# A hybrid gMLP and Mamba-2 layer on one core: low parts of the first operands on other engines, z tiles fetched one segment earlier, one norm three steps later

## Chip, core and metric

The kernel runs on one core of a Trainium2 chip. The metric is the device time of one execution in microseconds (us), taken on the core. Five engines work side by side, each with its own queue of instructions in a fixed order: TensorE (PE in the profile, its weight loads PEld), VectorE (DVE), ScalarE (ACT), GpSimd (POOL) and SyncE (SP), which here issues most of the DMAs.

## What is computed

One layer of a diffusion backbone on 2048 tokens of width 1024 with 256 context tokens, all in fp32:

```python
def _rms(x):
    x32 = x.astype(jnp.float32)
    y = x32 * lax.rsqrt(jnp.mean(x32 * x32, axis=-1, keepdims=True) + EPS)
    return y.astype(x.dtype)
...
    proj = h @ (w_in if with_output else w_in[:, 2 * GM_WIDTH:])
    ssd_in = proj[..., proj.shape[-1] - SSD_IN_WIDTH:]
    z, xbc, dt_raw = jnp.split(ssd_in, [SSD_WIDTH, SSD_WIDTH + CONV_CH], axis=-1)
    xbc = jax.nn.silu(_conv_centred(xbc, conv_w, conv_b))
```

A root-mean-square norm with a scale and a shift from the conditioning vector (adaLN) gives the operand h. One projection of h feeds a gated MLP and a bidirectional Mamba-2 scan over chunks of 128 tokens; the output of the scan is multiplied by the gate silu(z) and normed. A second projection, a gated residual, another adaLN norm, a SwiGLU feed-forward part with a hidden width of 2816, a second gated residual and a last norm with its own weight follow. The context tokens give only the states from which the scans start.

## The kernel before

Activations lie with the channels on the partitions, in tiles of 128 channels by 512 tokens. The 2048 tokens are two blocks of two such columns of tiles, so a block has two halves of 512 tokens. A product in fp32 is made of three matmuls on parts: each operand is split into a high part (rounded to the format that TensorE takes at full rate, fp32r) and a low part (the rest), and high by high, high by low and low by high are added in a PSUM bank (`mm3`, L228 to L231 where the low parts come late, L234 to L236 otherwise). Three PSUM banks (`mmp`) take the products of a unit of weights, five (`smp`) take the rest.

**Start (to about 100 us).** The block worked on first has halves x2 (tiles `x2s`) and x3 (`x3s`), and the context comes beside it (`hc`). For each of the eight tiles of a half, `put` (L985 to L988) makes the operand pair `actt`: ScalarE writes the high part, scale times x plus shift (L986); GpSimd writes the same in full fp32 over x (L987); VectorE subtracts the high part and writes the low part (L988). The norm of x3 needs the sum of eight squares: ScalarE squares (L316), GpSimd adds seven times (L318), TensorE sums over partitions with a matrix of ones (L322), ScalarE takes Ln and Exp (L252, L253), VectorE refines (L254 to L256), and x3 is multiplied by the result (L1009) ahead of its own `put`. Then TensorE works through units of weights with the two halves and the context: a unit's bank for one half takes 16 matmuls of high parts and 8 with the low part of the activation (L231).

**Scan stage (about 800 to 1530 us).** `y_out` is a generator in segments, run for 32 pairs of chunk and head group, with other generators between the segments: matmuls and first sums, then the adds, then the gate: a DMA brings the z tile (L822), VectorE multiplies (L823), ScalarE squares and sums along the row (L824). TensorE transposes the result (L831). Products of the output projection run in between; VectorE takes their banks (L932).

**Second feed-forward product and last norm.** `ffn2` goes through seven phases of 11 steps (12 matmuls in a step), phase 3 last but one and phase 4 last. Half 1 is complete after phase 3, half 0 after phase 4. VectorE adds the banks to the residual tile (L1289), which SP has loaded (L1287); squares are summed (L261, L264), and `final` (L1329 on) does the norm: ones matmul (L1332), Ln and Exp, eight products (L1336) and eight stores (L1337). `final` of half 1 is called a number of steps after phase 3 has ended, `due`, in the middle of phase 4.

A tile framework gives each engine its queue: what the program writes is taken through a scheduler that fixes the order of instructions on every engine before the run, and places the waits on semaphores. The order on the chip is then that of the queues.

Of the kernel before, what the change touches and what calls it, by code (L numbers as in the profile page):

```python
# [7 lines left out]
F32 = mybir.dt.float32  # L8
F32R = mybir.dt.float32r
I32 = mybir.dt.int32  # L10
AF = mybir.ActivationFunctionType
ALU = mybir.AluOpType
# [9 lines left out]
TB = 512  # L22
# [61 lines left out]
def kernel(ctx: ExitStack, tc: tile.TileContext, xT, ctxp, cc, crow, wad1, wad2, vecs, rows,  # L84
                             gmb, wall, wdt, gmw, csts, outT, dbg=None):
    nc = tc.nc
    V, S, G, PE, DMA = nc.vector, nc.scalar, nc.gpsimd, nc.tensor, nc.sync
# [16 lines left out]
    def tma():  # L104
        return tpa.tile([P, 520], F32, name="tma", tag="tma")
# [9 lines left out]
    def mmp():  # L115
        return psm.tile([P, TB], F32, name="mmp", tag="mmp")

    def smp():
        return pss.tile([P, TB], F32, name="smp", tag="smp")

    def actt():
        return ap_.tile([P, 2, TB], F32R, name="actt", tag="actt")

    def bc(ap, n):
        return ap.broadcast_to(list(ap.shape[:-1]) + [n])
# [4 lines left out]
    zscr = [tc.dram_tile([P, D], F32, name=f"zscr{i}") for i in range(NCH)]  # L130
# [179 lines left out]
        return hs  # L310

    def sum_sq(xs, n, eng=V):
        acc = None
        for x in xs:
            sq = tma()
            S.activation(sq[:, :n], x, AF.Square)  # L316
            if acc is not None:
                eng.tensor_tensor(out=acc[:, :n], in0=acc[:, :n], in1=sq[:, :n], op=ALU.add)  # L318
            else:
                acc = sq  # L320
        ps = smp()
        PE.matmul(ps[:, :n], lhsT=ones, rhs=acc[:, :n], start=True, stop=True)  # L322
        return rstd_of(ps, n, tma)
# [18 lines left out]
    x3s = [x3t[k // 2][:, (k % 2) * TB:(k % 2 + 1) * TB] for k in range(KT)]  # L342
# [9 lines left out]
    def scale(xs, rb, n, eng):  # L352
        for x in xs:
# [14 lines left out]
        out=a1, in0=m_sb[:, 8:16, :], scalar=1.0,  # L368
        in1=bc(vec[:, V_N1:V_N1 + 8].rearrange("p (a o) -> p a o", o=1), 2), op0=ALU.add, op1=ALU.mult)
# [3 lines left out]
                    scalar1=0.5, scalar2=None, op0=ALU.mult)  # L373
# [312 lines left out]
    zdone = [0]  # L686
# [110 lines left out]
    def y_out(st, c, g, ms):  # L797
        rc, Gt, hb = st["rc"], st["G"], st["hb"]
        h = hst[(0, g)]
        py, pf, pb = smp(), smp(), smp()  # L800
        PE.matmul(pf, lhsT=rc[:, R_C:R_C + P], rhs=h, start=True, stop=True)
        PE.matmul(pb, lhsT=rc[:, R_C:R_C + P], rhs=hb, start=True, stop=True)
        for e in range(8):
            PE.matmul(py[:, e * HD:(e + 1) * HD], lhsT=Gt[e // 4][:, (e % 4) * P:(e % 4 + 1) * P],
                      rhs=rc[:, R_X + e * HD:R_X + (e + 1) * HD], start=True, stop=True)
        ya, yb = tma()[:, :TB], hb
        V.tensor_tensor(out=h3(ya), in0=h3(pf), in1=hv(eac[:, c, g * 8:g * 8 + 8]), op=ALU.mult)
        V.tensor_tensor(out=h3(yb), in0=h3(pb), in1=hv(eac[:, c, 16 + g * 8:16 + g * 8 + 8]), op=ALU.mult)
        yield
        if c < NCH - 1:  # L810
            pS = smp()
            PE.matmul(pS, lhsT=rc[:, R_B:R_B + P], rhs=st["xd"], start=True, stop=True)
            G.tensor_tensor(out=h3(h), in0=h3(h), in1=hv(tot[:, c, g * 8:g * 8 + 8]), op=ALU.mult)
            V.tensor_tensor(out=h, in0=h, in1=pS, op=ALU.add)
        V.tensor_tensor(out=ya, in0=ya, in1=yb, op=ALU.add)
        V.tensor_tensor(out=ya, in0=ya, in1=py, op=ALU.add)
        G.tensor_tensor(out=h3(yb), in0=h3(rc[:, R_X:R_X + TB]), in1=hv(row[:, 64 + g * 8:64 + g * 8 + 8]), op=ALU.mult)
        V.tensor_tensor(out=ya, in0=ya, in1=yb, op=ALU.add)
        yield
        assert zdone[0] > min(g * 8 + c + 1, 15)  # L820
        zt = tma()[:, :TB]
        DMA.dma_start(zt, zscr[c][:, g * TB:(g + 1) * TB])  # L822
        V.tensor_tensor(out=ya, in0=ya, in1=zt, op=ALU.mult)  # L823
        S.activation(zt, ya, AF.Square, accum_out=ms)  # L824
        yield
        return ya
# [157 lines left out]

    def put(x, dst, n, a, sh):  # L985
        S.activation(dst[:, 0, n], x, AF.Identity, scale=a, bias=sh)  # L986
        G.tensor_scalar(out=x, in0=x, scalar1=a, scalar2=sh, op0=ALU.mult, op1=ALU.add)  # L987
        V.tensor_tensor(out=dst[:, 1, n], in0=x, in1=dst[:, 0, n].bitcast(F32), op=ALU.subtract)  # L988

    for k in range(KT):  # L990
        h = actt()
        put(x2s[k], h, slice(0, TB), a1[:, k, 0:1], m_sb[:, k, 0:1])
        hs[0].append(h)
    for i, t in enumerate(xcs):
        ks = slice(2 * i, 2 * i + 2)
        t3 = t.rearrange("p (a b) -> p a b", a=2)
        for k in range(2):
# [3 lines left out]
                        in1=rbc[:, CTX:NX2].rearrange("p (o b) -> p o b", o=1).broadcast_to([P, 2, 2]), op=ALU.mult)  # L1001
        V.tensor_tensor(out=t3[:, :, CTX:NX2], in0=t3[:, :, CTX:NX2], in1=bc(a1[:, ks, 0:1], 2), op=ALU.mult)
        V.tensor_tensor(out=t3[:, :, CTX:NX2], in0=t3[:, :, CTX:NX2], in1=bc(m_sb[:, ks, 0:1], 2), op=ALU.add)
        S.copy(hcp[i][:, :, 0, :], t3)
        V.tensor_tensor(out=hcp[i][:, :, 1, :], in0=t3, in1=hcp[i][:, :, 0, :].bitcast(F32), op=ALU.subtract)
    rb3 = sum_sq(x3s, TB, G)
    for k in range(KT):
        h = actt()
        V.tensor_tensor(out=x3s[k], in0=x3s[k], in1=rb3[:, :TB], op=ALU.mult)  # L1009
# [249 lines left out]
    def ffn2(blk, side):  # L1259
# [17 lines left out]
        def prep(n):  # L1277
            w = raw.pop(n)
            hi, lo = hl4(), hl4()
            split(w, hi, lo)  # L1280
            rdy[n] = (hi, lo)
# [9 lines left out]
        acc = [None, None]  # L1291
        due = None
# [5 lines left out]
        for n, (p, i) in enumerate(steps):  # L1298
            if n + LD < len(steps):
                load(n + LD)  # L1300
            if n + PP < len(steps):
                prep(n + PP)
            if i == 0:
                bank[p] = bank[1] if p in (6, 7, 4) else bank[5] if p == 3 else [mmp() if p == 1 and m < NPM else smp() for m in range(4)]
            hi, lo = rdy.pop(n)
            fst, lst, cont = i == 0 and p in (1, 2, 5), i == NK - 1, p not in (1, 2, 5)
            for m in range(4):
                ms_ = slice(TB + m * P, TB + (m + 1) * P)
                PE.matmul(bank[p][m], lhsT=hi[:, ms_], rhs=hi[:, A0], start=fst, stop=False, skip_group_check=cont)  # L1309
                PE.matmul(bank[p][m], lhsT=hi[:, ms_], rhs=lo[:, A0], start=False, stop=False, skip_group_check=cont)  # L1310
                PE.matmul(bank[p][m], lhsT=lo[:, ms_], rhs=hi[:, A0], start=False, stop=lst, skip_group_check=cont)  # L1311
            if i == NK - 1:
                for m in range(4):
                    upd(p, m)
                for m in range(4):
                    j, mm = {2: (0, m), 7: (1, 4 + m), 3: (1, m), 4: (0, 4 + m)}.get(p, (None, None))
                    if j is not None:
                        acc[j] = sq_acc(acc[j], x2[j, mm], t2, (G, V)[j] if p != 4 else V)
                if p == 3:
                    due = n + 3  # L1320
                if p == 4:
                    final(blk, 0, x2, acc[0])
            if n == due:
                final(blk, 1, x2, acc[1])
            next(side, None)
# [133 lines left out]
```

## Time and profile before

| | us |
|---|---|
| median of 3 runs | 2922.42 (2921.04 to 2922.88) |
| the profiled execution's own time | 2923.61 |
| its span in the profile | 2921.8 |
| TensorE busy | 2803.1 (96%) |
| VectorE busy | 1975.6 (68%) |
| ScalarE busy | 1274.2 (44%) |
| GpSimd busy | 645.4 (22%) |

The span runs from the first to the last instruction; 1.8 us of the execution's own time lie around it. Busy shares are means over the whole run: where time is lost is read from the timeline of a stage, in which every row has the start, the duration, the engine, the line, the operation with output and input, and in brackets the idle time before it and what ended it.

### The profile page before, as it was taken

What the parts mean: (1) busy time and instruction counts of PE and PEld (TensorE: products, weight loads), DVE (VectorE), ACT (ScalarE), POOL (GpSimd) and SP (SyncE); (2) the same over time, 40 slices, a digit from 0 to 9 for tenths busy, and PEclk for the clock granted to TensorE, in tenths of its full rate; (3) what the DMA queues carried; (4) which work ended last, traced back from release to release, by engine and by line L of the source; (5) the groups of instructions that cost most, each with busy time, mean ns of one, the idle gap of its engine ahead of it and who ended that gap; (6) DMA issues with size and microseconds to landing.
All of it is one profiled execution on the core that took longest, in us unless ns stands there. A gap on an engine that the chain in (4) does not pass through costs nothing. (4 is left out here: it accounts for less than half of the span.)

```text
span 2921.8 us, 36695 instructions
## 1 busy us (share of the span) xinstructions
PE 2803.1 (96%) x12478; PEld 2242.7 (77%) x12478; DVE 1975.6 (68%) x3007; ACT 1274.2 (44%) x2361; POOL 645.4 (22%) x555
## 2 busy tenths in 40 slices
PE   7999999999999998998979899999999999999997
PEld 2788778888677776776768688888887788888886
DVE  6776866886678888678676765555876544445556
ACT  4445343344356555444443533333554333333443
POOL 3200000200032233232202444444211222221000
PEclk8999999999999999999989999999999999999998
DMA  6232567743664678787658444445775423334654
GB/s 228 89 94 78 193 226 243 252 127 91 224 187 145 185 253 269 230 268 235 211 178 282 170 156 149 165 154 181 256 249 195 133 102 101 108 109 136 224 192 162
DMA packets 296743, 528.02 MB, mean 181 GB/s; under 512 B 28998, under 2 KB 89830, under 8 KB 296556
## 3 DMA queue, kind: packets, MB, share of 16 engines
q1 hardware_dynamic: 255756, 505.48, 53.0%
q10 hardware_dynamic: 40800, 20.21, 2.4%
q8 instruction: 98, 1.61, 0.2%
q14 instruction: 89, 0.73, 0.1%
HBM read 382.94 MB, written 142.64 MB: 180 GB/s over the span
## 5 line engine op out<-in xcount | busy, mean ns | idle before, releaser
L1065 DVE TENSOR_TENSOR hl<-w,hl 128x1024 fp32r<-128x1024 f32 x286 | 372.1, 1306 | 300.8 <-ACT hl L1064 129.5
L1064 ACT CAST hl<-w 128x1024 fp32r<-128x1024 f32 x286 | 298.8, 1048 | 423.1 <-PE smp L1311 150.0
L234 PE MATMUL mmp<-actt,whi 128*128 128x512 f32 x1120 | 455.7, 407 | 13.3 <-DVE tma L932 8.7
L236 PE MATMUL mmp<-actt,wlo 128*128 128x512 f32 x1120 | 442.1, 395 | 0.0
L235 PE MATMUL mmp<-actt,whi 128*128 128x512 f32 x1120 | 441.5, 394 | 0.2 <-DVE actt L898 0.2
L1179 PE MATMUL mmp<-hl,hl 128*128 128x512 f32 x704 | 276.5, 393 | 2.6 <-ACT t L1204 2.6
L1181 PE MATMUL mmp<-hl,hl 128*128 128x512 f32 x704 | 275.7, 392 | 1.0 <-DVE hl L1065 1.0
L1180 PE MATMUL mmp<-hl,hl 128*128 128x512 f32 x704 | 275.6, 392 | 0.0
L234 PEld LDWEIGHTS mmp<-actt,whi 128*128 128x128 f32 x1120 | 213.7, 191 | 62.0 <-DVE tma L932 9.7
L235 PEld LDWEIGHTS mmp<-actt,whi 128*128 128x128 f32 x1120 | 213.8, 191 | 47.0 <-issue 4.3
L236 PEld LDWEIGHTS mmp<-actt,wlo 128*128 128x128 f32 x1120 | 213.2, 190 | 46.0 <-issue 0.2
L234 PE MATMUL mmp<-whi,actt 128*128 128x512 f32 x512 | 208.9, 408 | 2.9 <-DVE tma L698 2.9
L1180 PE MATMUL smp<-hl,hl 128*128 128x512 f32 x528 | 208.5, 395 | 3.0 <-DVE hl L1065 3.0
L1181 PE MATMUL smp<-hl,hl 128*128 128x512 f32 x528 | 208.2, 394 | 2.5 <-DVE hl L1065 2.5
L1179 PE MATMUL smp<-hl,hl 128*128 128x512 f32 x528 | 209.8, 397 | 0.4 <-ACT hl L1064 0.4
L235 PE MATMUL mmp<-wlo,actt 128*128 128x512 f32 x512 | 206.4, 403 | 0.5 <-DVE wlo L221 0.5
L236 PE MATMUL mmp<-whi,actt 128*128 128x512 f32 x512 | 206.0, 402 | 0.0
L1071 DVE TENSOR_TENSOR t<-smp,t 128x512 f32<-128x512 f32 x88 | 60.5, 687 | 181.1 <-PE smp L1181 131.4
L787 POOL TENSOR_TENSOR tma<-tma 128x512 f32<-128x512 f32 x64 | 93.4, 1461 | 339.4 <-ACT tma L786 138.4
L456 DVE SCALAR_TENSOR_TENSOR tma<-xin,cw,tma 128x512 f32<-128x512 f32 x192 | 144.3, 751 | 25.5 <-ACT tma L454 19.3
L1179 PEld LDWEIGHTS mmp<-hl,hl 128*128 128x128 f32 x704 | 132.7, 189 | 32.5 <-ACT t L1204 3.0
L1071 POOL TENSOR_TENSOR w<-w 128x512 f32<-128x512 f32 x44 | 58.9, 1339 | 446.2 <-DVE hl L1065 290.8
(276 smaller groups left out, 5809.0 us busy)
## 6 DMA issues: line engine op xcount, KB each, us to landing
w<-in_wall_dram SPq DMA_DIRECT2D x110, 512.0 KB, 3.8
ws<-in_wall_dram SPq DMA_DIRECT2D x104, 512.0 KB, 5.0
ascr<-t SPq DMA_DIRECT2D x154, 256.0 KB, 3.9
w<-ascr SPq DMA_DIRECT2D x154, 256.0 KB, 3.3
tma<-fscr SPq DMA_DIRECT2D x128, 256.0 KB, 5.7
w<-wscr SPq DMA_DIRECT2D x88, 256.0 KB, 3.0
t<-x2scr SPq DMA_DIRECT2D x76, 256.0 KB, 4.1
w<-in_wall_dram SPq DMA_DIRECT2D x66, 256.0 KB, 3.1
```

Source lines behind the costliest of these rows:

```text
L234: PE.matmul(ps, lhsT=lh, rhs=rh, start=(i == 0), stop=False)
L235: PE.matmul(ps, lhsT=lh, rhs=rl, start=False, stop=False)
L236: PE.matmul(ps, lhsT=ll, rhs=rh, start=False, stop=(i == n - 1))
L456: V.scalar_tensor_tensor(out=acc[:, :n], in0=raw[:, j:j + n], scalar=cw[:, ch, j:j + 1], in1=acc[:, :n], op0=ALU.mult, op1=ALU.add)
L787: G.tensor_tensor(out=A, in0=A, in1=fb, op=ALU.mult)
L1064: S.copy(hi, x)
L1065: eng.tensor_tensor(out=lo, in0=x, in1=hi.bitcast(F32), op=ALU.subtract)
L1071: eng.tensor_tensor(out=o, in0=a, in1=b, op=ALU.add)
L1179: PE.matmul(ps, lhsT=hi[:, ms_], rhs=t[:, 0, :], start=first and k == 0, stop=False, skip_group_check=not first)
L1180: PE.matmul(ps, lhsT=hi[:, ms_], rhs=t[:, 1, :], start=False, stop=False, skip_group_check=not first)
L1181: PE.matmul(ps, lhsT=lo[:, ms_], rhs=t[:, 0, :], start=False, stop=k == 3, skip_group_check=not first)
```

## The change

Three edits. In `put` the low part is now made by VectorE (scale times x minus the high part, L993) and ScalarE (plus the shift, written as the low part, L994), and GpSimd has no part in it; the squares of x3 are summed before the first `put` (a new `sq_sum`, the first half of `sum_sq`, called with GpSimd), while the ones matmul and the rest (`sum_root`) stay where the whole was. The DMA of the z tile is issued in the first segment of `y_out` (L814) and no longer in the third. The norm of half 1 is due six steps after the end of phase 3, where it was three. Lines of the changed kernel lie 3 to 9 higher: L318 is L321, L322 is L328, L823 is L829, L1289 is L1296, L1332 is L1339, L1336 is L1343.

```diff
     def sum_sq(xs, n, eng=V):
+        return sum_root(sq_sum(xs, n, eng), n)
+
+    def sq_sum(xs, n, eng):
         acc = None
         for x in xs:
             sq = tma()
...
                 acc = sq
+        return acc
+
+    def sum_root(acc, n):
         ps = smp()
...
+        assert zdone[0] > min(g * 8 + c + 1, 15)
+        zt = tma()[:, :TB]
+        DMA.dma_start(zt, zscr[c][:, g * TB:(g + 1) * TB])
         ya, yb = tma()[:, :TB], hb
...
         yield
-        assert zdone[0] > min(g * 8 + c + 1, 15)
-        zt = tma()[:, :TB]
-        DMA.dma_start(zt, zscr[c][:, g * TB:(g + 1) * TB])
         V.tensor_tensor(out=ya, in0=ya, in1=zt, op=ALU.mult)
...
     def put(x, dst, n, a, sh):
         S.activation(dst[:, 0, n], x, AF.Identity, scale=a, bias=sh)
-        G.tensor_scalar(out=x, in0=x, scalar1=a, scalar2=sh, op0=ALU.mult, op1=ALU.add)
-        V.tensor_tensor(out=dst[:, 1, n], in0=x, in1=dst[:, 0, n].bitcast(F32), op=ALU.subtract)
-
+        V.scalar_tensor_tensor(out=x, in0=x, scalar=a, in1=dst[:, 0, n].bitcast(F32), op0=ALU.mult, op1=ALU.subtract)
+        S.activation(dst[:, 1, n], x, AF.Identity, bias=sh)
+
+    acc3 = sq_sum(x3s, TB, G)
...
-    rb3 = sum_sq(x3s, TB, G)
+    rb3 = sum_root(acc3, TB)
...
                 if p == 3:
-                    due = n + 3
+                    due = n + 6
```

The order of the queues moves with it. Three places follow.

**ScalarE, start, around the Ln of the norm of x3** (L1004, now L1011, is the high part of the context; `xin` here are tiles of x2, `whi` tiles of x3). Before:

```order
L986 ACTIVATE actt<-xin,m_sb,a_238 128x512 x2
L1004 CAST hc_488<-wlo 128x2x258
L1004 CAST hc_489<-wlo 128x2x258
L316 ACTIVATE tma<-whi 128x512 x6
L523 COPY xin<-mmp 128x512
L1004 CAST hc_490<-wlo 128x2x258
L252 ACT_TABLE_LOAD
L252 ACTIVATE tma<-smp,eps_t 128x512
```

Of the change:

```order
L994 ACTIVATE actt<-xin,m_sb 128x512 x3
L992 ACTIVATE actt<-xin,m_sb,a_238 128x512
L1011 CAST hc_488<-wlo 128x2x258
L1011 CAST hc_489<-wlo 128x2x258
L994 ACTIVATE actt<-xin,m_sb 128x512
L1011 CAST hc_490<-wlo 128x2x258
L1011 CAST hc_491<-wlo 128x2x258
L252 ACT_TABLE_LOAD
L252 ACTIVATE tma<-smp,eps_t 128x512
```

The squares L316 have gone ahead of all this, and the Ln now stands behind the last low part of x2 and all four parts of the context.

**ScalarE, start, from the parts of x3 to the copies that empty the context's banks** (L513 and L515, now L519 and L521). Before:

```order
L523 COPY xin<-mmp 128x512
L513 COPY xin<-mmp 128x2
L515 COPY tma<-mmp 128x256
L513 COPY xin<-mmp 128x2
L454 ACTIVATE tma<-tma,cw 128x256
L986 ACTIVATE actt<-whi,m_sb,a_238 128x512 x4
L220 CAST whi<-ws 128x1024 x2
L986 ACTIVATE actt<-whi,m_sb,a_238 128x512 x4
```

Of the change:

```order
L992 ACTIVATE actt<-whi,m_sb,a_238 128x512
L994 ACTIVATE actt<-whi,m_sb 128x512
L220 CAST whi<-ws 128x1024
L994 ACTIVATE actt<-whi,m_sb 128x512
L220 CAST whi<-ws 128x1024
L519 COPY xin<-mmp 128x2
L521 COPY tma<-mmp 128x256
L519 COPY xin<-mmp 128x2
```

The copies have moved from ahead of the sixteen parts of x3 to behind the last of them. On TensorE the two products with x3 that were interleaved now stand one whole unit after the other (16 high and 8 low matmuls, then again 16 and 8).

**VectorE, the end of the last phase of the last block** (`t_...` are residual tiles and squares, `mmp` and `smp` the banks of phase 4). Before:

```order
L1336 SCALAR_TENSOR_TENSOR t_22797<-t_22797,vec,t_23308 128x512
L1065 TENSOR_TENSOR hl_23408<-w_23369,hl_23407 128x1024
L1065 TENSOR_TENSOR hl_23424<-w_23388,hl_23423 128x1024
L1289 SCALAR_TENSOR_TENSOR t_23463<-mmp,m_sb,t_23463 128x512
L1289 SCALAR_TENSOR_TENSOR t_23466<-mmp,m_sb,t_23466 128x512
L1289 SCALAR_TENSOR_TENSOR t_23469<-mmp,m_sb,t_23469 128x512
L1289 SCALAR_TENSOR_TENSOR t_23472<-smp,m_sb,t_23472 128x512
L264 TENSOR_TENSOR t_22343<-t_22343,t_23475 128x512
L264 TENSOR_TENSOR t_22343<-t_22343,t_23478 128x512
```

Of the change:

```order
L1343 SCALAR_TENSOR_TENSOR t_22797<-t_22797,vec,t_23365 128x512
L1296 SCALAR_TENSOR_TENSOR t_23463<-mmp,m_sb,t_23463 128x512
L1296 SCALAR_TENSOR_TENSOR t_23466<-mmp,m_sb,t_23466 128x512
L264 TENSOR_TENSOR t_22343<-t_22343,t_23475 128x512
L264 TENSOR_TENSOR t_22343<-t_22343,t_23478 128x512
L1296 SCALAR_TENSOR_TENSOR t_23469<-mmp,m_sb,t_23469 128x512
L1296 SCALAR_TENSOR_TENSOR t_23472<-smp,m_sb,t_23472 128x512
```

The eight products of half 1 now stand directly ahead of the residual adds of half 0. On SP the order there is the same before and after: two loads of residual tiles, the eight stores of half 1, two more loads (tiles t_23469 and t_23472), and the stores of half 0. On TensorE the norm's matmul stands 36 matmuls later in each block.

## Rows read from the trace of the kernel before

**Rows 1.** Windows of 5 us: window, summed, PE, PEld, DVE, ACT, POOL busy, then TensorE's granted clock.

```profile
65.00:70.00 5.00, 1.57 (x3) 0.84 (x3) 4.76 (x9) 1.55 (x2) 3.69 (x9) 0.54 0.00 0
```

**Rows 2.** Timeline of TensorE, start.

```profile
68.43 2.07 PE L322 MATMUL smp<-tma,ones 128*128 128x512 f32 x2 [4.59 <-POOL tma L318]
...
98.68 0.28 PE L236 MATMUL mmp<-hc,wlo 128*128 128x258 f32 x1
98.80 0.39 PE L234 MATMUL mmp<-actt,whi 128*128 128x512 f32 x1
99.03 0.40 PE L235 MATMUL mmp<-actt,whi 128*128 128x512 f32 x1
```

**Rows 3.** Timeline of ScalarE, start.

```profile
47.62 2.92 ACT L986 ACTIVATE actt<-xin,m_sb,a 128x512 fp32r<-128x512 f32 x4
...
52.31 1.13 ACT L1004 CAST hc<-wlo 128x516 fp32r<-128x516 f32 x2
...
69.07 1.28 ACT L252 ACT_TABLE_LOAD   x1
70.55 0.69 ACT L252 ACTIVATE tma<-smp,eps_t 128x512 f32<-128x512 f32 x1 [0.19 <-PE smp L322]
...
81.79 1.05 ACT L220 CAST whi<-ws 128x1024 fp32r<-128x1024 f32 x1 [0.77 <-DVE actt L988]
```

**Rows 4.** Timeline of GpSimd, start.

```profile
43.59 1.26 POOL L318 TENSOR_TENSOR tma<-tma 128x512 f32<-128x512 f32 x1 [9.35 <-ACT tma L316]
46.17 12.26 POOL L987 TENSOR_SCALAR xin<-xin,a,m_sb 128x512 f32<-128x512 f32 x8 [1.32 <-ACT actt L986]
58.40 8.44 POOL L318 TENSOR_TENSOR tma<-tma 128x512 f32<-128x512 f32 x5
```

**Rows 5.** Timeline of VectorE, start.

```profile
54.45 7.90 DVE L988 TENSOR_TENSOR actt<-xin,actt 128x512 fp32r<-128x512 f32 x8
62.28 3.45 DVE L1005 TENSOR_TENSOR hc<-wlo,hc 128x516 fp32r<-128x516 f32 x2
...
71.78 0.70 DVE L1005 TENSOR_TENSOR hc<-wlo,hc 128x516 fp32r<-128x516 f32 x1 [1.91 <-ACT hc L1004]
...
75.17 0.69 DVE L256 SCALAR_TENSOR_TENSOR tma<-tma 128x512 f32<-128x512 f32 x1
...
92.33 0.69 DVE L988 TENSOR_TENSOR actt<-whi,actt 128x512 fp32r<-128x512 f32 x1 [0.59 <-POOL whi L987]
```

**Rows 6.** Waits of the whole run: engine, line, releaser, us in total, times, longest.

```profile
DVE tma L823 <- DMA tma<-zscr: 20.8, 9, 4.1
POOL tma L793 <- ACT tma L824: 10.8, 2, 7.8
```

**Rows 7.** Timeline of VectorE and TensorE, end of the scan stage.

```profile
1460.72 0.69 DVE L823 TENSOR_TENSOR tma<-tma 128x512 f32<-128x512 f32 x1 [4.09 <-DMA tma<-zscr]
...
1464.12 0.65 DVE L783 SCALAR_TENSOR_TENSOR tma<-tma,acs 128x128 f32<-128x128 f32 x2 [1.78 <-ACT tma L782]
...
1471.22 2.08 PE L802 MATMUL smp<-hb,rec_sb 128*128 128x512 f32 x2 [5.17 <-DVE tma L807]
```

**Rows 8.** Timeline of TensorE, VectorE and SP around the last norms.

```profile
2267.88 2.08 PE L1332 MATMUL smp<-t,ones 128*128 128x512 f32 x2 [5.78 <-DVE t L264]
...
2879.50 1.02 PE L1332 MATMUL smp<-t,ones 128*128 128x512 f32 x2
...
2888.05 5.38 DVE L1336 SCALAR_TENSOR_TENSOR t<-t,vec,t 128x512 f32<-128x512 f32 x8
...
2893.84 0.95 SPq L1287 DMA_DIRECT2D t<-x2scr  x2
...
2902.36 0.75 DVE L1289 SCALAR_TENSOR_TENSOR t<-smp,m_sb,t 128x512 f32<-128x512 f32 x1
...
2906.15 2.07 PE L1332 MATMUL smp<-t,ones 128*128 128x512 f32 x2 [3.83 <-DVE t L264]
```

**Rows 9.** DMA issues: count, size of each, median us from issue to landing.

```profile
t<-x2scr SPq DMA_DIRECT2D x76, 256.0 KB, 4.1
```

## The prediction

> **What bounds the kernel now.** The table of engines comes first: TensorE is busy 96% of the span, so only what shortens or lengthens its idle time, or the time in which it has a low clock, can move the end. The timeline of TensorE, read for its bracketed idle times, then says where that is. Three places touch the change. At the start TensorE waits for operands until 98.80 us; from there its matmuls follow each other every 0.23 us [rows 2]. In the scan stage it has single waits, as the 5.17 us at 1471.22 [rows 7]. At each end of the second feed-forward product the last norm waits for VectorE, 5.78 and 3.83 us [rows 8]. The norm that is moved did not wait (2879.50, no bracket) [rows 8]. So I ask of each edit when TensorE gets its operand there, and follow the queues back from it.
>
> **The start.** Removed: 16 products of GpSimd (eight took 12.26 us) [rows 4]. Added: 16 instructions of ScalarE of the size of its high part, 2.92 / 4 = 0.73 us each [rows 3]. The 16 low parts on VectorE change form only; a scalar_tensor_tensor of that size takes 0.69 us [rows 5], what L988 takes alone [rows 5]. Moved: seven adds of GpSimd, from between 43.59 and 68.4 us to one piece from 43.6 us on.
>
> What those adds cost VectorE is the first thing to see. Two L1005 took 3.45 us, 1.72 each, while GpSimd added; alone one took 0.70 [rows 5, 4]. The eight L988 took 7.90 us: up to 58.40, while GpSimd did its one-input L987, 3.95 us hold 5.7 of them at 0.69; the other 3.95 us, beside adds, hold 2.3 at 1.72. So a product of GpSimd costs VectorE nothing, an add some 1.72 - 0.69 = 1.03 us. Moving the adds moves that cost, and doesn't remove it: VectorE has work of the same kind without a pause in either place.
>
> *Until the norm of x3.* I walk the queues of the change with these durations. VectorE begins at 45.2 us and has 39 instructions up to x2's last L993, 14.8 us of work (eight of 0.69, the rest smaller pieces, most of the context), and 2.9 us of waits for ScalarE's high parts: without hold-ups it is there at 62.9 us. ScalarE adds 0.73 for the low part, two context casts at 1.13 / 2 each, a table load of 1.28, and the Ln of 0.69: it ends at 66.7. Six adds fall beside VectorE's work: 6 x 1.03 = 6 us more, 72.7. Before, the Ln ended at 70.55 + 0.69 = 71.24 [rows 3], when it waited for TensorE's sum, which waited 4.59 us for GpSimd's last add [rows 2]. The sum is early now (the adds end near 56), but the Ln has a longer queue ahead of it: **+1.4 us**. From the Ln to the refined factor (before 75.86) [rows 5] nothing changes.
>
> *From there to the last low part.* Before: 75.86 to 93.02, 17.16 us, each low part waiting for a product of GpSimd [rows 5]. Now ScalarE is the limit: 0.62 for the first multiply, 16 x 0.73 and one weight cast of 1.05 [rows 3] make 13.4: **-3.8 us**.
>
> *From there to the full stream.* Before, 93.02 to 98.80, 5.8 us, since the two products of x3 were interleaved and both nearly done. Now the second one starts after the first, and its bank is freed by copies that ScalarE does behind its last low part and a cast: about 1.6 us, then 24 matmuls at 0.23 (5.45), then 24 of the context at 0.12 (2.9) [rows 2]: 9.95, **+4.2 us**.
>
> The sum is 1.4 - 3.8 + 4.2 = +1.8, say **+2 us** for the start. Its ends: with no hold-up at all, 6 us less, -4; with 1.26 us per add (one alone) [rows 4], 1.4 more, and with part of the late product at the low clock, as between 65 and 70 us, where TensorE was busy 1.57 of 5 us and the granted clock was 0.54 (nearly all at 1.2 GHz) [rows 1], about 1.9 more: +5.
>
> The Trainium skill (SBUF — State Buffer, section "SBUF: two separate sides") has a rule that speaks against this part: a VectorE instruction with two SBUF inputs and a GpSimd one that reads SBUF take a shared pair of ports in turn, and the loser is blocked for the other's whole instruction. The rows of L1005 agree in kind (1.72 against 0.70). By the plain mean of the L988 (0.99 each, 0.30 lost) six adds would cost 1.8 us and the start would come out at -2.2; by the rule, with the whole 1.26 each, at +3.3.
>
> **The z tiles.** No instruction is added; 32 DMAs are issued earlier. VectorE waited for z 9 times of 32, 20.8 us in all [rows 6]. On TensorE that hardly shows. The longest, 4.09 us at 1460.72, is followed by a wait of VectorE for ScalarE of 1.78 us at 1464.12, for scan factors that came by a DMA of their own [rows 7]; a VectorE that gets there sooner waits longer there, and TensorE's 5.17 us at 1471.22 stay. The z DMA of a pair moves up 0 to 8 places in SP's queue, mostly 2 to 4, past other loads; SP issues in the order of its queue, so where it waits for a store to be ready the z tile still waits. I take **-0.5 us**. Ends: -5, the whole of that one stall; +4, half of the longest wait that this tile ring shows, 7.8 us on a slot [rows 6], should the longer life of the z tile hold one up.
>
> **The norm three steps later.** TensorE loses nothing at the old place, so nothing is won there. What is moved is queued ahead of other work. In the last block the norm comes 36 matmuls, 36 x 0.227 = 8.2 us, after 2879.50. Its eight products began at 2888.05 with a weight split of VectorE ahead of them that now stands earlier (1.2 less): about 2895.0, done at 2900.4. Eight stores follow on SP, one per product. Behind them, in the same queue, stand two loads of residual tiles, issued at 2893.84 before [rows 8] and near 2900.8 and 2901.2 now. At 4.1 us to landing [rows 9] the tiles are there at 2904.9 and 2905.3; before, VectorE used the last one at 2902.36 [rows 8]. Two residual adds (0.7 each), a square (0.63) and the last sum (0.69) lead to the ones matmul at 2907.8 against 2906.15 [rows 8]: **+1.6 us**. In block 0 the same two loads have the same order behind the stores; the wait of 5.78 us at 2267.88 [rows 8] covers part of it, as GpSimd's late work ended last there: **+0.9**. Together **+2.5**; ends +1 (the loads land as VectorE's own work ends) and +5 (both land 1.2 us later, as beside eight stores they may).
>
> **Sum.** +2 - 0.5 + 2.5 = **+4 us** on the profiled execution's 2923.61 us, 2921.8 of span and 1.8 around it: 2927.6. That execution stands 1.2 us above the median of the runs, 2922.42; so the forecast is **2926.4 us**. A change of 0.2%, 5.8 us, is about what a measurement can tell from none: the forecast is within it.
>
> **Rivals.**
> - *Faster: GpSimd is what bears the hold-ups.* If adds wait for VectorE and not the other way, the start gives -4, and if z frees the stall at 1471.22, -5; with +1 for the norm: -8, **2914.4 us**. For it: the adds also took longer beside VectorE (8.44 / 5 = 1.69, against 1.26) [rows 4], so both pay. Against: L1005's 1.72. 0.2.
> - *Slower: the late product of x3 runs at the low clock.* Place: 88 to 98 us, where TensorE has had little but single matmuls since the factor. It decides if the granted clock there is near a half when the bank comes free; price +5 for the start. With the other two terms as they are, +7: **2929.4 us**. For it: 0.54 between 65 and 70 us [rows 1] after a stretch as thin. 0.2.
> - *Slower: the loads behind the stores.* Each lands late by 2 us more than reckoned, in both blocks: +5 for the norm, +6.5 in all, **2928.9 us**. For it: the order of SP. Against: 4.1 us is the median of 76 such loads [rows 9]. 0.1.
> - *The edits don't do what they say.* z still lands late where SP is held: its term is 0, and the sum stays within the band. It is part of the forecast, 0.5.
>
> **How the numbers follow.** Within 0.2% (2916.6 to 2928.3): 0.5, the forecast. Faster by more: 0.2, the first rival. Slower by more: 0.3, the second and the third. The range that leaves out 2 in 10 reaches from 2915 (nearly the first rival) to 2931 (above the last two).
>
> **What would show it.** Right: L993 beside adds near 1.7 us, eight GpSimd products gone, the Ln ending near 72.7, the last low part of x3 near 90.7, the full stream from about 100.7 us; no VectorE wait for z of over a microsecond, with TensorE's waits in the scan stage as they were; the last L1339 near 2907.8 with the residual loads issued after 2900. Wrong: the full stream starting before 97 us or after 103, or TensorE's idle time in the scan stage changing by more than 3 us in sum, which would mean that the new order, and not a wait that I named, sets the time.

## The result and the profile after

The changed kernel takes 2942.32 us (median of 6, 2940.88 to 2947.12) against 2921.73 us for the kernel before on the same chip (median of 6, 2919.67 to 2927.88): ratio 1.0071 [1.0058, 1.0084], 20.6 us slower. The forecast was 2926.4 us, within a range that ended at 2931: the time lies outside it, on the slower side. The profiled execution is the longest of its six, 2947.12 us with a span of 2945.3, so its trace shows some 5 us more than the median run lost.

Where the time went is seen by numbering TensorE's matmuls, 12478 in either trace, and taking for each the start after less the start before. This lag is -1.1 us at 100 us, +1.8 at 1000, +8.4 at 1150, +12.8 at 1300, +17.4 at 1500, +20.6 from 1700 to 2050, +21.2 at 2300 and at 2900; the span is 23.5 us longer. So the scan stage (1000 to 1700 us) takes 19 and the tail 2.3. Block 0's norm shows 1.2 at its ones matmul, of which 0.6 is left at 2300. The start's -1.1 and the 2.9 us between 100 and 1000 are too small to read from one trace: in e5 below, whose queues are those of the kernel before, the lag wanders between 0 and 5 us up to 2260 us (2.7 at 100) and the span is 0.1 longer. The line of the engines, with busy time, share and instructions, shows nothing of the loss:

```profile
PE 2810.1 (95%) x12478; PEld 2246.2 (76%) x12478; DVE 1973.6 (67%) x3007; ACT 1286.2 (44%) x2377; POOL 619.7 (21%) x539
```

**The start.** The timeline of VectorE after (start, us, engine, line, operation, tiles, shape, count; in brackets the idle time ahead and its releaser):

```profile
46.33 0.74 DVE L993 SCALAR_TENSOR_TENSOR xin<-xin,a,actt 128x512 f32<-128x512 f32 x1
46.99 1.25 DVE L1007 TENSOR_TENSOR wlo<-wlo,tma 128x4 f32<-128x4 f32 x1
...
56.06 0.15 DVE L1009 TENSOR_TENSOR wlo<-wlo,a 128x4 f32<-128x4 f32 x1
56.40 1.22 DVE L1010 TENSOR_TENSOR wlo<-wlo,m_sb 128x4 f32<-128x4 f32 x1
...
58.57 0.15 DVE L1007 TENSOR_TENSOR wlo<-wlo,tma 128x4 f32<-128x4 f32 x1
58.64 0.74 DVE L993 SCALAR_TENSOR_TENSOR xin<-xin,a,actt 128x512 f32<-128x512 f32 x1
...
66.31 0.75 DVE L993 SCALAR_TENSOR_TENSOR xin<-xin,a,actt 128x512 f32<-128x512 f32 x1 [1.80 <-ACT actt L992]
```

GpSimd's six adds run meanwhile, as its timeline says:

```profile
46.48 11.11 POOL L321 TENSOR_TENSOR tma<-tma 128x512 f32<-128x512 f32 x6 [1.88 <-ACT tma L319]
```

A VectorE operation on 128x4 takes 0.15 us when nothing holds it and 1.25 when an add does. Five of that size were held so, 1.1 us each, and one of 128x32 (L397, 1.26 us): 6 to 6.5 us in all. None of them was one of the low parts (L993), on which the prediction had put the price; only one of those came before the adds were done, and it had begun, at 46.33, before the first of the six adds (46.48). The adds took 1.85 us each, against 1.26 for one alone [rows 4]. ScalarE, which needs those low parts, then stands still:

```profile
59.42 2.19 ACT L994 ACTIVATE actt<-xin,m_sb 128x512 fp32r<-128x512 f32 x3 [6.35 <-DVE xin L993]
...
70.28 0.69 ACT L252 ACTIVATE tma<-smp,eps_t 128x512 f32<-128x512 f32 x1
...
87.22 0.72 ACT L994 ACTIVATE actt<-whi,m_sb 128x512 fp32r<-128x512 f32 x1
```

The Ln ends at 70.97 us (before 71.24 [rows 3]) and the last low part of x3 at 87.94. TensorE's timeline gives the rest, and the windows its clock (summed, busy of PE, PEld, DVE, ACT, POOL, granted clock, DMA share, GB/s):

```profile
57.65 1.73 PE L328 MATMUL smp<-tma,ones 128*128 128x512 f32 x2 [1.98 <-POOL tma L321]
...
89.25 0.50 PE L228 MATMUL mmp<-actt,whi 128*128 128x512 f32 x1 [0.76 <-ACT xin L519]
...
97.72 0.39 PE L234 MATMUL mmp<-actt,whi 128*128 128x512 f32 x1
```

```profile
80.00:85.00 5.00, 3.90 (x9) 2.28 (x8) 5.00 (x9) 5.00 (x9) 0.00 (x0) 0.50 0.00 0
85.00:90.00 5.00, 4.03 (x15) 2.46 (x14) 3.30 (x4) 5.00 (x11) 0.21 (x1) 0.97 0.10 20
90.00:95.00 5.00, 5.00 (x24) 4.10 (x24) 4.06 (x8) 2.31 (x4) 0.17 (x1) 1.00 0.58 193
```

The full stream begins at 97.72 us, against 98.80 [rows 2]. The granted clock was 0.50 (1.2 GHz) while the first product of x3 waited for its operands one by one, and 1.00 when the late second one ran.

**The scan stage.** Waits between 800 and 1560 us (engine, tile, line, releaser, us in total, times, longest), after, then before:

```profile
ACT tma L788 <- DMA tma<-fscr: 149.1, 42, 10.2
ACT tma L830 <- DVE tma L829: 54.8, 18, 5.7
SPq L814 <- POOL tma L793: 23.1, 6, 6.5
SPq L814 <- DMA sscr<-tma: 9.8, 2, 6.4
SPq L814 <- DMA tma<-fscr: 9.6, 3, 4.8
```

```profile
ACT tma L824 <- DVE tma L823: 107.4, 26, 7.8
ACT tma L782 <- DMA tma<-fscr: 82.9, 37, 5.9
```

VectorE's wait for z [rows 6] is gone. But two others have changed. SP waits 65.3 us in 24 places at the z load itself (L814; three of its rows stand above) for a slot of the tile ring, 15.7 us in 11 before. And ScalarE's two large waits have changed places: it waited most for the gated product that it squares (L824, now L830), and waits most now for the scan factors (L782, now L788). The sum of all its waits in the window hardly moves, 366.7 us before and 373.2 after. SP's hardly moves either, 525.4 and 536.5 us. TensorE's waits of this stage (800 to 1600 us) grow from 48.7 us in 22 to 61.0 in 26. In the records of its granted clock, 0.50 stands for 58.0 us of 1000 to 1700 before and for 68.3 after; an estimate from that is 5 us of work put off, so that waits and clock together make most of the 19. Either share alone is loose: e5 has 56.0 us of waits and 51.2 us at 0.50, with the span of the kernel before. Two of the longer waits after:

```profile
1393.58 1.11 PE L837 MATMUL smp<-ident,tma 128*128 128x128 f32 x4 [6.14 <-DVE tma L829]
1488.19 2.08 PE L808 MATMUL smp<-hb,rec_sb 128*128 128x512 f32 x2 [5.85 <-DVE tma L816]
```

The second is the stall of 5.17 us at 1471.22 [rows 7], which has stayed. VectorE no longer waits for z ahead of it, and waits longer for ScalarE's factors in its place, 3.24 us where it was 1.78 [rows 7]:

```profile
1477.44 0.65 DVE L789 SCALAR_TENSOR_TENSOR tma<-tma,acs 128x128 f32<-128x128 f32 x2 [3.24 <-ACT tma L788]
```

**The tail.** Timelines of SP and of TensorE after:

```profile
2909.92 6.81 SPq L1294 DMA_DIRECT2D t<-x2scr  x2
2917.17 5.25 SPq L1344 DMA_DIRECT2D out_dram<-t  x8
2922.47 1.32 SPq L1294 DMA_DIRECT2D t<-x2scr  x2
```

```profile
2929.64 2.07 PE L1339 MATMUL smp<-t,ones 128*128 128x512 f32 x2 [6.14 <-DVE t L264]
```

Less the 21.2 us that TensorE had already lost, the last ones matmul is at 2908.4 (before 2906.15 [rows 8]) and waits 6.14 instead of 3.83 us.

### The profile page after: what moved, and what is told of

Its sections match the earlier page's. It is cut to its first block, busy times and chain, and to the rows that moved or that the text cites. A ratio compares the mean times of both kernels' runs of the same rounds, so it can differ in the third digit from the quotient of the medians.

```text
span 2945.3 us, 36689 instructions
## 1 busy us (share of the span) xinstructions
PE 2810.1 (95%) x12478; PEld 2246.2 (76%) x12478; DVE 1973.6 (67%) x3007; ACT 1286.2 (44%) x2377; POOL 619.7 (21%) x539
## 5 line engine op out<-in xcount | busy, mean ns | idle before, releaser
L789 DVE SCALAR_TENSOR_TENSOR tma<-tma,acs 128x128 f32<-128x128 f32 x256 | 105.0, 432 | 82.1 <-ACT tma L788 80.3
```

## The experiments

Ratios are against the kernel before on the same chip, with a 95% interval.

### Each edit alone

e1 has the first two parts of the diff only (squares first, new `put`), e2 only the z tile's move, e3 only `due = n + 6`, e4 all but the z tile's move.

> The first edit alone (low parts by VectorE and ScalarE, squares first); z tiles and the norm as before. Theory Z (the loss is the z tiles': their early DMA waits for a slot of the tile ring in SP's queue, and the loads of scan factors stand behind it): within 3 us of before, full stream of TensorE at the start about 1 us earlier, scan stage as before. Rival O (the first edit makes the scheduler put all queues in a new order, and the scan stage loses by that): 12 to 18 us slower than before, most of it between 1000 and 1400 us.

> The z tiles alone. Theory Z: 13 to 18 us slower than before, ScalarE's waits for scan factors (fscr) near 150 us in the scan stage against 83, SP waiting for slots ahead of the z DMA. Rival O: within 3 us of before.

> The later norm alone. Both theories: 3 to 4 us slower than before, 1.4 of it at the norm between the blocks and about 2.3 at the end, where the last two residual loads are issued behind eight stores. A third theory (the norm costs nothing by itself and its loss in the changed kernel comes with the shifted order): within 1 us of before.

> The change without the z tiles. Theory Z: 1 to 6 us slower than before, the sum of the two single edits. Rival O: 16 to 21 us slower, nearly the whole loss of the change.

| run | us | before | ratio |
|---|---|---|---|
| e1, start | 2916.71 | 2920.44 | 0.9985 [0.9976, 0.9995] |
| e2, z | 2933.33 | 2920.44 | 1.0045 [1.0028, 1.0062] |
| e3, norm | 2926.37 | 2920.44 | 1.0021 [1.0012, 1.0030] |
| e4, start and norm | 2923.36 | 2920.44 | 1.0002 [0.9991, 1.0012] |

The start gains 3.7 us, the norm loses 5.9, and z loses 12.9. The product of the three ratios is 1.0051; the whole change has 1.0071, so some 6 us come only with all three together. That rest is within what the intervals leave. Most of it goes with the granted clock, 0.977 in the mean of the changed kernel's runs and 0.980 in e2's: time multiplied by granted clock, in the mean of the runs, is 2876 us for the changed kernel and 2875 for e2, against 2863 for e4 and 2864 for the kernel before. What lowered the clock is not shown. e2 shows the picture of the full change: SP waits 63.2 us in 23 places at the z load, and ScalarE's rows are

```profile
ACT tma L782 <- DMA tma<-fscr: 148.9, 42, 10.6
ACT tma L824 <- DVE tma L823: 55.5, 18, 5.6
```

### What of the start gains

e11 is the new `put` with the squares at their old place, e12 the squares first with the old `put`.

> Low parts by VectorE and ScalarE, the squares of x3 in their old place; SP's order is that of the kernel before. Theory L (the gain of the first edit, 4 us, is GpSimd's product going, as each low part of x3 waited for one): 1 to 4 us faster than before, the last low part of x3 earlier than 93.0 us. Rival Q (the gain is the early sum of squares): within 1.5 us of before or slower.

> The squares of x3 summed first, the low parts as before with GpSimd's products. Theory L: within 2 us of before or slower, since GpSimd does adds and products by turns and the low parts of x2 come later. Rival Q: 2 to 5 us faster than before.

e11: 2923.52 against 2925.58, 0.9997 [0.9987, 1.0007]. e12: 2920.07, 0.9981 [0.9971, 0.9991]. The gain comes from the early sum of squares, -5.5 us; in e12's trace the full stream starts at 95.57 us, against 98.80 [rows 2]. Taking GpSimd's sixteen products away gives nothing that can be measured, alone or on top of it (e1 against e12).

### The norm: what the two loads wait for

e3's waits of SP between 2885 and 2912 us, and its timeline of SP:

```profile
SPq L1287 <- PE smp L1332: 9.6, 1, 9.6
SPq L1287 <- DVE t L256: 6.1, 1, 6.1
```

```profile
2896.02 5.24 SPq L1337 DMA_DIRECT2D out_dram<-t  x8
2901.31 1.30 SPq L1287 DMA_DIRECT2D t<-x2scr  x2
```

The first two of the four loads of residual tiles (L1287) wait for slots that the norm itself frees: its sum, matmul L1332, then its factor, L256. The last two (2901.31) have no wait of their own in e3's trace; they stand behind the eight stores, and each store waits for its product. The third residual add, 4.1 us after its load was issued, is the one that waits:

```profile
2905.45 0.75 DVE L1289 SCALAR_TENSOR_TENSOR t<-mmp,m_sb,t 128x512 f32<-128x512 f32 x1 [1.97 <-DMA t<-x2scr]
2906.90 1.49 DVE L264 TENSOR_TENSOR t<-t,t 128x512 f32<-128x512 f32 x2
```

e8 takes the stores of half 1 out of SP's queue, in e3's kernel:

```diff
-            DMA.dma_start(outT[k * P:(k + 1) * P, ts_], x)
+            (DMA if j == 0 else S).dma_start(outT[k * P:(k + 1) * P, ts_], x)
```

> The later norm alone, with the eight stores of half 1 issued by ScalarE in both blocks, so that the last two residual loads don't stand behind them. Theory S (the loss at the end is those loads' place): the last ones matmul waits under 4.5 us against 6.1 with the norm alone, and the time is 1.5 to 3 us below the norm alone. Rival V (the loss is VectorE's: eight products stand ahead of the residual adds): as the norm alone, 5 to 6 us slower than before.

2935.77 against 2924.49, 1.0034 [1.0024, 1.0045]: worse, not better. All four loads now stand together on SP, and the third waits for a slot until one of the stores that ScalarE issues has landed. Its timeline of SP, its waits of SP (2885 to 2920 us), and its timelines of TensorE and VectorE:

```profile
2892.33 11.71 SPq L1287 DMA_DIRECT2D t<-x2scr  x4
```

```profile
SPq L1287 <- DMA out_dram<-t: 3.5, 1, 3.5
```

```profile
2912.91 2.08 PE L1332 MATMUL smp<-t,ones 128*128 128x512 f32 x2 [7.02 <-DVE t L264]
```

```profile
2908.07 0.75 DVE L1289 SCALAR_TENSOR_TENSOR t<-mmp,m_sb,t 128x512 f32<-128x512 f32 x1 [2.60 <-DMA t<-x2scr]
2909.78 3.07 DVE L264 TENSOR_TENSOR t<-t,t 128x512 f32<-128x512 f32 x4
```

The loads do come sooner. TensorE was 3.6 us later here than in e3 ahead of the norm; less that, the last two are issued 2 us earlier than in e3, and the third add begins at 2904.5 against 2905.45. But VectorE's queue has come out in another order: four sums (L264, 3.07 us) stand behind the last add, where e3 has two (1.49 us), and the matmul waits longer for them. In block 0 it is the same: the third add begins at 2260.91 (e3: 2263.79), yet the ones matmul waits 7.49 us (5.41), as sums and weight splits stand behind the adds. So e8 does not clear the place behind the stores: it takes some of that delay away, and loses more by the new order on VectorE.

### z: the slots of the ring

e5 was to take the z tile's slot early and load late:

```diff
+        zt = tma()[:, :TB]
         ya, yb = tma()[:, :TB], hb
```

> The z tile takes its slot of the tile ring in the first segment, as in the change, but its DMA is issued in the third, as before; SP's order is that of the kernel before. Theory W (the loss is SP's: the early DMA waits there for the slot, some 60 us in sum, and the loads of scan factors stand behind it): within 4 us of before, ScalarE's wait for scan factors near 83 us. Rival R (the loss is the ring's: a z tile that holds its slot longer makes other tiles wait for theirs, whoever issues the DMA): 8 to 13 us slower than before.

2923.10 against 2924.49, 0.9992 [0.9982, 1.0003]. The framework gives a slot at the first use, so the queues are those of the kernel before: a second measurement of it, and no word on slots. (Instruction by instruction, all five queues in its trace are those of the kernel before.) e10, e13, e14 and e15 change the ring itself (`NTMA`, 14 before): to 13; to 15, with the room from the small tiles (`sml`, 64 wide, made 32, as in e16 to e18 too; that alone was not run); to 15 with z early; to 15 with the first edit.

> The kernel before with 13 slots in the tile ring in place of 14, nothing else. Theory W says that what a load needs is a free slot when SP comes to it: with one slot less SP waits for slots as with the early z tile, and the time rises by 8 us or more. Rival (slots are not scarce; only the z tile's order matters): within 3 us of before.

> The kernel before with 15 slots in the tile ring (room for it from narrower tiles of small sums, 32 columns for 64, of which 16 are used). Theory R (slots of the ring are what the scan stage lacks): 4 to 15 us faster than before. Rival O (14 slots are enough when z is late; the loss comes from the order of the queues): within 3 us of before.

> The z tiles alone, as in the change, with 15 slots. Theory R: the early z has its slot, within 5 us of the kernel before with 15 slots, no slower than before. Rival O: 10 us or more slower than the kernel before with 15 slots.

> The first edit of the change alone, with 15 slots: the sum of both, if they are independent. Theory R: 6 to 18 us faster than before. Rival O: 2 to 6 us faster than before.

| run | us | before | ratio | SP at the z load | ScalarE for factors |
|---|---|---|---|---|---|
| e10, 13 slots | 2946.98 | 2925.58 | 1.0072 [1.0055, 1.0089] | 22.9 | 69.4 |
| e13, 15 slots | 2920.63 | 2926.69 | 0.9979 [0.9967, 0.9992] | 12.3 | 83.7 |
| e14, 15 slots, z early | 2930.63 | 2926.69 | 1.0016 [1.0006, 1.0026] | 46.8 | 129.5 |
| e15, 15 slots, first edit | 2915.70 | 2926.69 | 0.9967 [0.9955, 0.9980] | 15.0 | 82.6 |

One slot less costs 21 us and one more gives 6, each with the order of the queues that the scheduler then makes. But z early costs 10 us with 15 slots too (2930.63 - 2920.63), and with 13 slots ScalarE's wait for factors is not longer but shorter. e15 is 11 us faster than the kernel before.

### z: the wait in the queue

e6 and e7 give z one buffer of its own, beside 13 slots, with the load at its old and its new place; e16 gives it two, beside 13; e17 one, beside all 14; e9 has the ring's tile, with the load issued by GpSimd.

```diff
+        zt = ztp.tile([P, TB], F32, name="zt", tag="zt")
+        DMA.dma_start(zt, zscr[c][:, g * TB:(g + 1) * TB])
```

> The z tile has one buffer of its own, the ring 13 slots for the rest; DMA in the third segment, as before. It is the ground for the next run. Both theories: within 8 us of before either way, since one slot less and one tile less nearly cancel; VectorE's waits for z near 20 us.

> As the run with the own buffer, but the DMA is issued in the first segment, as in the change; ScalarE's and the ring's order are the same in both. Theory W: without a slot of the ring to wait for, SP is not held and the time is within 3 us of the late one, VectorE's waits for z gone. Rival P (the place itself costs: an early z load stands ahead of the loads of scan factors and they come later): 8 us or more slower than the late one, ScalarE's wait for scan factors 50 us or more above.

> The z tiles in the first segment, as in the change, but their DMAs are issued by GpSimd and no longer by SP; slot and place in the program are those of the change. Theory W (SP is held at the z DMA and the loads of scan factors behind it come late): the loss of 13 us of the z tiles alone is gone, 3 us faster to 4 us slower than before, ScalarE's wait for scan factors back from 149 to under 100 us; GpSimd, busy a fifth of the time, takes the waits. Rival T (the early z transfer itself, or the slot it holds, slows the rest): 8 us or more slower than before.

> z early in two buffers of its own, ring of 13 for the rest. The grounds are the ring of 13 with z in it (0.7% slower than before) and one own buffer with a ring of 13 (1.05% slower, SP waiting 56 us for that buffer). Theory W (waiting at the z DMA in an in-order queue is the loss): SP's wait at the z DMA under 15 us, at most 0.7% slower than before, 8 us or more below the run with one own buffer. Rival P (the early place and the order that comes with it are the loss, slots or not): as with one own buffer, 1.0% or more slower than before.

> z early in one buffer of its own, ring of 14 for the rest. Theory W: SP waits 50 us or more for that buffer, 8 us or more slower than before. Rival R (the ring's slots are the loss; z is out of the ring and the rest has one tile less to share it with): no slower than before, like the ring of 15.

| run | us | before | ratio | waits at the z load | ScalarE for factors |
|---|---|---|---|---|---|
| e6, own buffer, 13 slots, old place | 2952.64 | 2924.49 | 1.0105 [1.0085, 1.0124] | SP 55.8 | 153.6 |
| e7, the same, new place | 2955.84 | 2924.49 | 1.0109 [1.0083, 1.0134] | SP 53.4 | 148.7 |
| e16, two buffers, 13 slots | 2956.24 | 2922.47 | 1.0119 [1.0102, 1.0135] | SP 46.3 | 147.6 |
| e17, one buffer, 14 slots | 2934.84 | 2922.47 | 1.0046 [1.0025, 1.0066] | SP 53.8 | 149.3 |
| e9, by GpSimd | 2938.00 | 2925.58 | 1.0047 [1.0029, 1.0065] | GpSimd 13.9 | 156.4 |

e6 and e7 can't be told apart, and e6, expected within 8 us of before, is no ground for e7: their queues are the same but for one pair of neighbours swapped on SP and on ScalarE, and z is asked for early in both, a median of 18.6 us ahead of its use (before 5.6, e2 9.0). By ratio both stand some 10 us above e10 (1.0072), which has 13 slots as well. e16 was to load without a wait; it issues still earlier, 41.8 us ahead, and waits again. e17 uses no slot of the ring for z and loses as much as e2, so the ring's slots are not needed for the loss. e9 does not hold SP at z, and loses as much too. But e17 holds SP, and e9 takes a slot: each leaves one of the two. The last run has neither. It is e17 with the load issued by ScalarE, which reads the buffer last and so has next to nothing to wait for (0.38 us at most in the stage, in its trace):

```diff
-        DMA.dma_start(zt, zscr[c][:, g * TB:(g + 1) * TB])
+        S.dma_start(zt, zscr[c][:, g * TB:(g + 1) * TB])
```

> As the kernel with one own buffer for z beside the ring of 14, but ScalarE issues the load of z. ScalarE itself reads the buffer last, and the load stands in its queue right behind that square in most pairs, so the load has no buffer to wait for, takes no slot of the ring, and no other load stands behind it on SP. Theory H (what costs is a wait for a slot or buffer in front of other work: SP held, or a ring slot taken early): without both the loss goes; ratio 0.997 to 1.001 (2914 to 2925 us where the kernel before has 2922), ScalarE waits under 100 us for scan factors. Theory O (z early is what costs, by its transfer beside the other loads or by the new order of the queues): the loss stays, ratio at least 1.003 (+8 us), and ScalarE waits 130 us or more for scan factors. A term of its own that both leave open: the issue itself on ScalarE, 32 times, up to 1 us each where ScalarE's chain is the limit.

2937.14 against 2926.55, 1.0042 [1.0026, 1.0058]. The loss stays. Its waits in the scan stage, and its timeline of ScalarE around one of the loads:

```profile
ACT tma L782 <- DMA tma<-fscr: 141.6, 42, 9.8
ACT zt L824 <- DVE tma L823: 57.5, 15, 7.7
```

```profile
1111.27 0.19 ACT L824 ACTIVATION_READ_ACCUMULATOR zt<-tma 128x1 f32 x1
1115.54 0.40 ACT L782 ACTIVATE tma<-tma,nacs 128x128 f32<-128x128 f32 x1 [4.08 <-DMA tma<-fscr]
1115.61 0.34 ACTq L808 DMA_DIRECT2D zt<-zscr  x1
```

No queue is held at z and no ring slot is taken, and one issue takes ScalarE 0.34 us; yet the two waits stand as in e2, and TensorE's waits of the stage are 63.2 us in 24. So theory H falls, with one reservation: the 32 issues are 11 us of ScalarE's time that no other run has, and what they cost was not measured. What e18 shares with e2, e9, e14 and e17 is a z that is asked for early, and queues that are no longer those of before. With the z tile alone moved, 94 of VectorE's 3007 instructions stand outside the order that e2's queue shares with that of before, 80 of ScalarE's 2447, 56 of SP's 1718 (29 of them z loads), 9 of TensorE's 12478 and none of GpSimd's. Two pieces of ScalarE's (- before, + e2):

```
+L824 ACTIVATE tma,sml<-tma 128x512
 L697 ACTIVATE tma<-mmp 128x512
 L833 COPY tma<-smp 128x512
 L834 DMA sscr_152<-tma 128x4x128
 L220 CAST whi<-ws 128x1024
-L824 ACTIVATE tma,sml<-tma 128x512
 L782 ACTIVATE tma<-tma,nacs 128x128 x4
...
-L782 ACTIVATE tma<-tma,nacs 128x128 x2
-L824 ACTIVATE tma,sml<-tma 128x512
-L782 ACTIVATE tma<-tma,nacs 128x128
-L784 ACTIVATE tma<-rec_sb,dt_sb 128x128 x3
...
+L782 ACTIVATE tma<-tma,nacs 128x128 x4
+L824 ACTIVATE tma,sml<-tma 128x512
+L784 ACTIVATE tma<-rec_sb,dt_sb 128x128 x4
```

The gated product, its square and the next pair's factor work stand anew in some of the 32 pairs. The swap of ScalarE's two waits goes with an early z: it stands in all nine kernels with one (the changed one, e2, e6, e7, e9, e14, e16, e17, e18) and in none of the others. So does a piece of the order: in these nine the squares of pairs 17 to 20, 22 and 23 stand one to four factor instructions (L782) further back, in none of the others. But the nine have not one order: VectorE's queue in e18 has 166 instructions outside that of before and 139 outside that of e2. Whether the loss comes from one of the moved instructions, and which, or from 32 transfers that run beside others, was not tried: no run has the early load with the old order, or the new order with a late load. The loads of scan factors took a median of 5.7 us to landing before, and 5.3 to 6.0 in e2, e9, e17 and e18, which speaks little for the transfers.

## Why the prediction was wrong

**The z tiles: the step that failed.** It is "No instruction is added; 32 DMAs are issued earlier." The term was -0.5 us with ends of -5 and +4; the measured one is +12.9 alone, and some 20 us in the full change (1.0071 against 1.0002 in e4). The sentence holds for the program's text and not for the queues: the step priced a DMA that moves while all else keeps its place, and the order of the queues was used only at the start and at the norm. What the runs showed in its place is a loss of 10 to 13 us wherever z is early and the ring has its 14 slots, whoever issues the load and whichever buffer it fills (e2, e9, e17, e18), together with a new order on four engines at least. That the order is the cause is likely and not shown. The queue of SP was walked, but only for what z gains there. That other loads stand behind a z that waits for its slot, 65.3 us in sum, was left out; e18 shows that the loss comes without it too. The upper end of +4, half of one wait for a slot, was a bound on a single stall, while what came comes in several steps: in e2's trace TensorE's lag grows from 0.6 us at 1000 to 10.8 at 1500, with no wait longer than the 8.7 us that before has as well. The stall at 1471.22 behaved as reckoned: it stayed, as VectorE waited longer for ScalarE in place of z. The text's own sign of being wrong, TensorE's idle time in the scan stage changing by over 3 us, came (+12.3). Its bound was too narrow, as e5, with the queues of the kernel before, shows +7.3 without a loss, and its reading, "that the new order, and not a wait that I named, sets the time", fits but is not shown.

**The start: right in its parts, wrong in sign.** The hold-ups were counted well: 6 adds, 6 to 6.5 us measured against 6 x 1.03. Yet the Ln ended at 70.97 instead of 72.7, as VectorE was done with x2 at 67.06 instead of 68.9: it waited 1.9 us (reckoned 2.9), and its work without hold-ups came to 13.6 us (reckoned 14.8). The step "a product of GpSimd costs VectorE nothing" does not hold either: in the trace of before, five VectorE operations that ran beside L987 took some 0.4 us longer than their like took alone. Two rows from there, the second of them held:

```profile
50.10 0.15 DVE L1000 TENSOR_TENSOR wlo<-wlo,tma 128x4 f32<-128x4 f32 x1
50.56 0.58 DVE L1002 TENSOR_TENSOR wlo<-wlo,a 128x4 f32<-128x4 f32 x1
```

By that estimate, taking the products away gives VectorE some 2 us back, which the sum left out. From the refined factor (75.57) to the last low part took 12.4 us (reckoned 13.4), and from there to the full stream 9.8 (9.95). So +2 became -1.1 in this trace, and -3.7 in e1's runs. Which of the two moves pays was wrong: the walk gave the gain to the freed products (-3.8) and a loss to the moved adds, where e12 shows a gain of the moved adds and e11 none of the products that can be measured. In e12 the Ln ends at 68.59 us.

The Trainium skill ("SBUF — State Buffer", section "SBUF: two separate sides") says that the loser is blocked for the other's whole instruction. The rows agree in kind and nearly in size: 1.1 us for operations of 0.15 us, against 1.26 for an add alone. Both sides paid, 1.1 us for VectorE and 1.85 - 1.26 = 0.59 for GpSimd per add, so the loser changed by turns.

**The norm: right mechanism, too small.** Forecast +2.5. e3's trace gives 1.4 in block 0 and 2.3 at the tail (the changed kernel's 0.6 and 2.3), against +0.9 and +1.6; e3's runs give +5.9 [3.5, 8.8]. In e3 the last two loads were issued at 2901.31 and 2902.00 (reckoned 2900.8 and 2901.2), landed in the 4.1 us of the reckoning, and the ones matmul came at 2908.44 (2907.8). The term that was mis-sized is the +2.5, by 1.2 us in that trace; the rest of the 5.9 is not explained, and 3.7 lies inside the interval.

**The rivals.** The late product of x3 ran at 1.00, not at the low clock: it fell. GpSimd alone bearing the hold-ups fell. The loads behind the stores landing 2 us late fell: they took 4.1 us in e3's trace; that e3's runs come near its price of +5 is luck. None had the price of z; slower had 0.3, all of it on other places.

## What to carry to other kernels

Where a scheduler orders the queues, moving one load of a program moved some 240 instructions on four engines: read the difference on every engine of that stage before pricing the move at what the moved instruction does. A load that its user waits 20.8 us for in all, off the path that TensorE waits on, is no reason to fetch it earlier. And measure a slot of a full tile ring early: here one is worth 6 us upwards and 21 downwards, the latter more than any of the three edits alone.

## What the runs showed of the hardware

A GpSimd add of 128x512 held one VectorE instruction each time, for about 1.1 us (128x4: 0.15 to 1.25 us; 128x516, L1005: 0.70 to 1.72 [rows 5]), and let the others of that stretch pass at their usual time (L1005 of the changed kernel, 128x256, 0.47 us). GpSimd's products of the kernel before (L987) held some by 0.4 us (128x4: 0.15 to 0.58). Single executions of the kernel before reach from 2914.37 to 2932.57 us in the record, and go with the granted clock: of 103, the 13 at 0.978 or less have a median of 2928.4 us, the 11 at 0.982 or more 2918.8. So a term of 2 us can't be read from one time, nor, as e5's lag shows, from one trace, unless its wait is named.
